# The scheduler's table of write tails, 300 cycles longer for VectorE and ScalarE, in a hybrid scan and MLP block

## The chip, the core and the metric

The kernel runs on one core of one Trainium2 chip. A core has five engines with queues of their own, each of which takes its instructions in the order of the program: PE (TensorE, matrix products, with its weight loads shown as PEld), DVE (VectorE), ACT (ScalarE), POOL (GpSimd) and SP (SyncE), which issues the transfers here. They wait for each other by semaphores. The metric is the time of one execution on the device in microseconds; lower is better.

## The reference

One layer of a generator's trunk works on 256 context tokens and 2048 latent tokens of width 1024. A modulated norm and one projection over all 2304 tokens give the columns of four mixers (mLSTM, RWKV-7, GLA, Gated DeltaNet; four heads each). Each mixer runs a forward and a backward scan over chunks of 64 tokens, 36 chunks in all, the context first. Their outputs go through one output projection, a gated residual, a second norm, an MLP with a squared ReLU and a last norm.

```python
mod_x = jax.nn.silu(c) @ ada_w[layer] + ada_b[layer]
...
hx = _rms(x, norm1_w[layer]) * (1 + scale1_x) + shift1_x
hc = _rms(ctx, norm1_w[layer]) * (1 + scale1_c) + shift1_c
z = (jnp.concatenate([hc, hx], axis=1) @ w_in[layer]).astype(jnp.float32)
z_ml, z_rw, z_gl, z_gd = _split(z, (ML_W, RW_W, GL_W, GD_W))
mixed = jnp.concatenate([
    _mlstm_mixer(z_ml, ...), _rwkv_mixer(z_rw, ...),
    _gla_mixer(z_gl, ...), _gdn_mixer(z_gd, ...)], axis=-1)
x = x + gate1_x * (mixed[:, n_ctx:] @ w_out[layer])
x = x + gate2_x * _mlp(_rms(x, norm2_w[layer]) * (1 + scale2_x) + shift2_x, ...)
...
return _rms(x, final_norm_w)
```

Two of the scans (RWKV-7 and Gated DeltaNet) solve a unit triangular system of 64 x 64 for each chunk, head and direction before their state can run:

```python
sol = lax.linalg.triangular_solve(-m_ab, rhs, left_side=True, lower=True, unit_diagonal=True)
...
def step(s, xs):
    w_c, u_c, a_c, k_c, v_c, ge = xs
    u_t = u_c + jnp.einsum('bhck,bhkv->bhcv', w_c, s)
```

## The kernel before

All dense products are made in three passes over split numbers (high by high, high by low, low by high), so a weight goes from its load `w_f` to `w_hi` on ACT and `w_lo` on POOL or DVE, and an activation to `hh` and `hl`.

**Stages.** Tokens are projected in five rounds (`round_`). A round begins with `make_h` (L533): for each of eight slices of 128 features, `xh` is loaded, multiplied by the norm's factor `rbr` on POOL, scaled on ACT, copied to `hh` on ACT, and `hl` is the rest on DVE; then PE makes the first product `ps_z`. After it come gates, the Gated DeltaNet's keys, the scalars, the RWKV columns (with `l2r` and `abrk` on POOL) and the columns of the other two. What the scans need goes to scratch in DRAM (`x_fm`, `x_tm`, `x_rows`, `x_gat`), from where a scan group (`group`) loads one chunk and one direction, runs its steps `ps_R`, `ps_U`, `ps_S`, `ps_att`, `ps_ym`, `ps_ylgr` and updates the state `St`. Four products for gates (`out_gates`), each with a `make_h` of its own, follow the rounds; a tail of output projection and MLP (`ps_o`, `ps_f`, `ps_a`) for four blocks of 512 tokens ends the program. 24 more groups stand in it.

**Solves.** `solve` serves four units (two chunks each). A `solve_prep` loads factors from `x_fm`, makes `ps_n` on PE and stores the system to `x_sN`. `find` loads it back (`s_s_b<-x_sN`) and inverts it in 31 steps of a product `s_t` and a subtraction into `s_s_x`, each on the result of the one before, on POOL (seven of the solves) or on DVE (solves of the last round, called `beside`). A `solve_post` makes two blocks of `ps_s` with ACT copies and stores the inverse to `x_t`, which the groups read. `s_s_b` and `s_s_x` are one buffer each, shared with the loads `adaw` of round 0's modulation and with `fill` (L349), which stores columns of ones into `x_tm`, four bytes at a time.

**What sets the order.** The program's text is interleaved by hand: a generator yields the pieces of a round, and `interleave` puts queued solves and groups between them.

```python
f = (i + 1 - lo * n) / ((hi - lo) * n)
want = min(len(steps), int(len(steps) * f)) if f > 0 else 0
...
r = _run(nc, [arrays], core_ids=[0])
```

On this the list scheduler of the tile framework works: it keeps a clock for each engine by tables of costs, and issues next what is ready first by these clocks. So the order on each engine, and nothing else of the program, depends on the tables. `transfers` (L1898) sets three entries of the tables for the time of scheduling and puts them back: the fixed cost of an SP transfer, its delay, and the bytes per ns of a DMA engine. The table the change adds to them gives, by kind of write of DVE and ACT, the cycles after an operation's end before the scheduler takes its result to be readable by another instruction.

Of the kernel before, what the change touches and what calls it, by code (L numbers as in the profile page):

```python
# [1897 lines left out]
@contextmanager  # L1898
def transfers():

    SP = mybir.EngineType.SP
    new = {"HWDGE_FIXED_OVERHEAD_NS": {**TRN2Spec.HWDGE_FIXED_OVERHEAD_NS, SP: 825},
           "DGE_DMA_DELAY": {**TRN2Spec.DGE_DMA_DELAY, SP: 1400},
           "DMA_BUS_BYTES_PER_NS_PER_ENGINE": 16.0}
    old = {k: getattr(TRN2Spec, k) for k in new}
    for k, v in new.items():
        setattr(TRN2Spec, k, v)
    try:
        yield
    finally:  # L1910
        for k, v in old.items():
            setattr(TRN2Spec, k, v)
# [15 lines left out]
```

## Time and profile before

| what | before |
|---|---|
| median of 3 runs | 4183.04 us (4180.95 to 4185.43) |
| the profiled execution | 4181.71 us |
| its span | 4179.9 us |
| mean granted clock of PE | 0.875 of full speed |
| busy: PE, DVE, ACT, POOL | 3462.1, 2490.3, 1403.3, 1464.4 us |
| moved by DMA | 592.66 MB, 142 GB/s on average |

By its landmarks in the trace the span falls into round 0 (to about 330 us), rounds 1 to 4 (to 1777), a stretch between two of the gates' dense pieces (to 1916 with its last hops), the rest of the gates (to 2280) and the tail. In the rows of the profile that follow, a timeline row gives the start and the duration in us, the engine, the line, the operation with what it writes and reads, and in brackets how long the engine had been idle and what released it. A window row gives, for each engine, the us in which it was busy and the number of instructions, then PE's granted clock, the busy share of the DMA engines and GB/s.

### The profile page before, as it was taken

The numbers are of one execution on the slowest core, as the hardware profiler recorded it, in microseconds if no ns is written. First come the engines' busy times: TensorE is split into PE (matmuls) and PEld (weight loads), VectorE is DVE, ScalarE is ACT, GpSimd is POOL, SyncE is SP. The second block draws the span as 40 slices with busy tenths as digits, with TensorE's granted clock in tenths as the row PEclk, the third lists the DMA queues.
The fourth block names the chain that finished last, engine by engine and source line by source line (L and its number), as shares of the span: only waits on it lengthen the run. The fifth ranks groups of instructions, "written<-read, shape, count | busy, mean of one in ns | idle before, by whom it ended". The sixth has DMA issues, their size and how long they took to land.

```text
span 4179.9 us, 75082 instructions
## 1 busy us (share of the span) xinstructions
PE 3462.1 (83%) x29082; PEld 2807.3 (67%) x29082; DVE 2490.3 (60%) x5259; ACT 1403.3 (34%) x2544; POOL 1464.4 (35%) x1682
## 2 busy tenths in 40 slices
PE   6465877867777876658896999999999999999998
PEld 5344666656556765547785777777778777877786
DVE  6673866764776585536865556567754464445444
ACT  3334334434433433323332323233322332233222
POOL 3221834552626253502242333334322232223222
PEclk9667978877887876768898999999999999999999
DMA  5568478657686864647777444454532333232322
GB/s 205 108 180 149 116 157 194 143 131 146 153 150 160 187 144 124 171 121 193 212 212 195 124 135 148 138 171 142 175 95 96 106 102 115 96 98 91 104 96 86
DMA packets 610372, 592.66 MB, mean 142 GB/s; under 512 B 286384, under 2 KB 487168, under 8 KB 610016
## 3 DMA queue, kind: packets, MB, share of 16 engines
q1 hardware_dynamic: 610016, 587.87, 53.9%
q8 instruction: 229, 3.75, 0.4%
q14 instruction: 127, 1.04, 0.1%
HBM read 463.78 MB, written 123.92 MB: 141 GB/s over the span
## 4 chain that ended last, share of the span: by engine, by line
PE 42%; DVE 4%; issue 1%; POOL 1%; ACT 1%; DMA 1%; SPq 0%; POOLq 0%; DVEq 0%; ACTq 0%
PE ps_a L240 17%; PE ps_f L240 15%; PE ps_o L240 4%; PE ps_ylgr L229 1%; PE ps_z L212 1%; PE ps_S L229 1%; PE ps_att L240 1%; DVE h2l L193 1%; DVE relu L185 1%; PE ps_R L229 1%; SPq L201 0%; PE ps_ym L229 0%; PE ps_yT L248 0%; PE ps_ml L240 0%; POOL yall L185 0%
## 5 line engine op out<-in xcount | busy, mean ns | idle before, releaser
L185 POOL TENSOR_TENSOR w_lo<-w_f,w_hi 128x1024 fp32r<-128x1024 f32 x213 | 513.9, 2413 | 1232.8 <-ACT w_hi L198 1144.1
L198 ACT ACTIVATE w_hi<-w_f 128x1024 fp32r<-128x1024 f32 (+1 forms) x427 | 448.5, 1051 | 878.1 <-PE ps_a L240 387.1
L240 PE MATMUL ps_a<-ah,w_hi 128*128 128x512 f32 x1024 | 408.0, 403 | 8.0 <-ACT ah L198 8.0
L240 PE MATMUL ps_f<-h2l,w_hi 128*128 128x512 f32 x1024 | 402.8, 394 | 8.7 <-DVE h2l L193 8.7
L185 DVE TENSOR_TENSOR w_lo<-w_f,w_hi 128x1024 fp32r<-128x1024 f32 (+1 forms) x214 | 275.0, 1285 | 222.4 <-ACT w_hi L198 218.2
L240 PE MATMUL ps_f<-h2h,w_hi 128*128 128x512 f32 x1024 | 404.4, 395 | 3.5 <-ACT w_hi L198 2.7
L240 PE MATMUL ps_a<-al,w_hi 128*128 128x512 f32 x1024 | 406.2, 397 | 1.0 <-DVE al L185 1.0
L240 PE MATMUL ps_f<-h2h,w_lo 128*128 128x512 f32 x1024 | 405.5, 396 | 1.1 <-DVE w_lo L185 1.1
L240 PE MATMUL ps_a<-ah,w_lo 128*128 128x512 f32 x1024 | 399.9, 398 | 0.0
L240 PE MATMUL ps_z<-hh,w_hi 128*128 128x512 f32 (+3 forms) x760 | 301.7, 403 | 73.7 <-ACT hh L198 34.2
L193 DVE SCALAR_TENSOR_TENSOR x1T<-ps_a,modv,x1T 128x512 f32<-128x512 f32 x256 | 188.0, 749 | 259.6 <-PE ps_a L240 258.9
L240 PE MATMUL ps_z<-hh,w_lo 128*128 128x512 f32 (+3 forms) x760 | 299.4, 395 | 21.2 <-DVE w_lo L185 11.0
L240 PE MATMUL ps_z<-hl,w_hi 128*128 128x512 f32 (+3 forms) x760 | 298.3, 393 | 2.1 <-DVE hl L185 1.9
L185 DVE TENSOR_TENSOR relu<-relu 128x512 f32<-128x512 f32 x128 | 188.4, 1473 | 113.0 <-ACT relu L198 112.9
L212 PE MATMUL ps_z<-w_hi,hh 128*128 128x256 f32 x672 | 210.3, 315 | 36.0 <-ACT hh L198 21.9
L240 PEld LDWEIGHTS ps_a<-ah,w_hi 128*128 128x128 f32 x1024 | 191.2, 189 | 64.7 <-ACT ah L198 16.5
L240 PEld LDWEIGHTS ps_z<-hh,w_hi 128*128 128x128 f32 (+1 forms) x760 | 155.2, 206 | 111.5 <-ACT hh L198 37.5
L240 PEld LDWEIGHTS ps_f<-h2l,w_hi 128*128 128x128 f32 x1024 | 193.9, 189 | 51.7 <-DVE h2l L193 10.7
L240 PEld LDWEIGHTS ps_f<-h2h,w_hi 128*128 128x128 f32 x1024 | 194.0, 190 | 46.0 <-ACT w_hi L198 4.4
L240 PEld LDWEIGHTS ps_a<-ah,w_lo 128*128 128x128 f32 x1024 | 193.4, 189 | 45.5 <-issue 0.3
L240 PEld LDWEIGHTS ps_a<-al,w_hi 128*128 128x128 f32 x1024 | 193.6, 189 | 44.8 <-DVE al L185 1.2
L240 PEld LDWEIGHTS ps_f<-h2h,w_lo 128*128 128x128 f32 x1024 | 193.9, 189 | 43.5 <-DVE w_lo L185 1.9
(430 smaller groups left out, 7976.9 us busy)
## 6 DMA issues: line engine op xcount, KB each, us to landing
w_f<-w SPq DMA_DIRECT2D x256, 512.0 KB
w_f<-wg SPq DMA_DIRECT2D x90, 512.0 KB
tm<-x_tm SPq DMA_DIRECT2D x144, 259.5 KB
kc<-x_fm SPq DMA_DIRECT2D x64, 448.0 KB
adaw<-ada SPq DMA_DIRECT2D x48, 512.0 KB
rw<-x_rows SPq DMA_DIRECT2D x144, 160.0 KB
w_f<-wp SPq DMA_DIRECT2D x44, 512.0 KB
w_f<-wout SPq DMA_DIRECT2D x32, 512.0 KB
```

The costliest lines, as they stand in the source:

```text
L185: return (e or self.V).tensor_tensor(out=o, in0=a, in1=b, op=op)
L193: return self.V.scalar_tensor_tensor(o, a, s, b, op0, op1)
L198: return self.S.activation(o, a, f, bias=bias, scale=scale)
L212: i = self.T.matmul(o, l, r, start=k == 0, stop=k == len(mms) - 1)
L229: i = self.T.matmul(t.t[rows, cols], l, r, start=not prev, stop=not any(left[q] for q in quarters), skip_group_check=True)
L240: return self.T.matmul(o, l, r, start=start, stop=stop)
```

## The change

A fourth table is set while the program is scheduled. Each of its eight entries, all of DVE or ACT, is raised by 300 cycles.

```diff
     new = {"HWDGE_FIXED_OVERHEAD_NS": {**TRN2Spec.HWDGE_FIXED_OVERHEAD_NS, SP: 825},
            "DGE_DMA_DELAY": {**TRN2Spec.DGE_DMA_DELAY, SP: 1400},
-           "DMA_BUS_BYTES_PER_NS_PER_ENGINE": 16.0}
+           "DMA_BUS_BYTES_PER_NS_PER_ENGINE": 16.0,
+
+           "TIMELINE_SIM_WRITE_TAIL_CYCLES": {k: v + 300 for k, v in TRN2Spec.TIMELINE_SIM_WRITE_TAIL_CYCLES.items()}}
     old = {k: getattr(TRN2Spec, k) for k in new}
     for k, v in new.items():
         setattr(TRN2Spec, k, v)
```

The instructions are the same in number and kind on every engine (PE 20456 matmuls in the order's count, DVE 5213, ACT 2546, POOL 1687, SP 2641); their order differs on all five. The mean place of an instruction moves by 85 on PE, 31 on DVE, 14 on ACT, 19 on POOL and 24 on SP. From about 3100 us of the trace of before on, the order is the same. Solves and scan groups stand earlier among the rounds, by 15 to 70 of PE's rows, and dense products later by 8 to 30, until the third of the gates' products, where both orders meet again.

**SP, end of round 0.** In the order of before, the four stores of ones by `fill` (`x_tm<-s_s_x 64x36x1`) stand behind the last load of `adaw` and the first weights `w_f` of the next product, and ahead of the loads of round 1's first solve (`s_s_b<-x_fm`) and of the next gate's weights:

```order
L201 DMA adaw<-ada 128x1024
L201 DMA x_tm<-tm 128x2x64
L201 DMA kc<-x_fm 128x128
L201 DMA ff<-x_fm 128x128
L201 DMA kc<-x_fm 128x256
L201 DMA kc<-x_fm 128x128
L201 DMA x_tm<-tm 128x2x128 x4
L201 DMA w_f<-wp 128x1024 x2
L201 DMA x_tm<-s_s_x 64x36x1 x4
L201 DMA s_s_b<-x_fm 128x2x128 x3
L201 DMA kc<-x_fm 128x256
L201 DMA s_s_x<-x_bg_90 64x2x256 x2
```

In the order of the change they stand among the stores of round 0's RWKV columns:

```order
L201 DMA adaw<-ada 128x1024
L201 DMA mf_bi<-x_msc_93 16x64
L201 DMA x_fm<-abrk 128x3x128
L201 DMA x_rows_89<-mf_re 4x4x64 x2
L201 DMA x_tm<-st 256x1x128
L201 DMA x_tm<-st 128x1x128
L201 DMA x_tm<-vt 256x1x64
L201 DMA x_tm<-vt 128x1x64
L201 DMA x_tm<-s_s_x 64x36x1
L201 DMA x_gat<-s_2243 256x1x128
L201 DMA x_gat<-s_2243 128x1x128
L201 DMA x_tm<-s_s_x 64x36x1 x3
```

The last `adaw` is SP's row 215 in the one and 184 in the other; the stores of ones moved from row 223 to rows 192 and 195.

**POOL, the last `find` on this engine.** In the order of before it begins when all `abrk` of round 4 and two updates of the state are behind it:

```order
L185 TENSOR_TENSOR abrk<-rmix,E 128x3x64
L1024 COPY reg<-E 128x3
L185 TENSOR_TENSOR w_lo<-w_f,w_hi 128x1024
L185 TENSOR_TENSOR s_17072<-vt,bon 128x4x64
L185 TENSOR_TENSOR s_17072<-s_17072,rgn 128x4x64
L185 TENSOR_TENSOR St<-St,rw 128x128
L185 TENSOR_TENSOR St<-St,reg 128x128
L185 TENSOR_TENSOR St<-St,rw 128x128
L185 TENSOR_TENSOR St<-St,reg 128x128
L1302 MEMSET s_s_x 128x1024
L1303 MEMSET s_s_x 128x32
L185 TENSOR_TENSOR s_t<-s_s_b,s_s_x 128x31
```

In the order of the change it begins behind the third-last and last `l2r`, with three `abrk` still to come:

```order
L1002 MEMSET E 128x3
L185 TENSOR_TENSOR abrk<-rmix,E 128x3x64
L1024 COPY reg<-E 128x3
L185 TENSOR_TENSOR l2r<-l2m,mhalf 128x6
L1302 MEMSET s_s_x 128x1024
L185 TENSOR_TENSOR St<-St,rw 128x128
L185 TENSOR_TENSOR St<-St,reg 128x128
L1303 MEMSET s_s_x 128x32
L185 TENSOR_TENSOR w_lo<-w_f,w_hi 128x1024
L185 TENSOR_TENSOR l2r<-l2m,mhalf 128x6
L185 TENSOR_TENSOR s_t<-s_s_b,s_s_x 128x31
L185 TENSOR_TENSOR s_s_x<-s_s_x,s_t 128x31
```

The `find` moved ahead of three `abrk`, of the bonus terms and of state updates; the eight `xh` of the first gates, which stand inside its last third before, stand behind it now. Elsewhere on POOL, `xh` rows come to stand inside other `find`s: of the rows of a `find`, 13 stand between the first and the last `xh` of round 3 and 7 between those of the gates before, and after 10 in round 1, 13 in round 2 and 18 in round 4. Up to the last `xh` of these three, 22, 13 and 49 rows of the `find` have gone by.

**PE, between the gates' second and third dense product.** In the order of before, the dense product `ps_z` ends and two blocks of `ps_s` of a `solve_post` follow, the first of four posts between here and the next `ps_z`, 132 rows on:

```order
L212 MATMUL ps_z<-w_lo,hh 128x256
L212 MATMUL ps_z<-w_hi,hl 128x256
L247 MATMUL ps_col<-pack,mf_m 64x32 x2
L247 MATMUL ps_col<-pack,mf_bi 64x16 x2
L240 MATMUL ps_s<-s_s_b 32x32 x16
L247 MATMUL ps_col<-pack,mf_ee 64x16 x2
L240 MATMUL ps_s<-s_s_x 32x32 x16
L229 MATMUL ps_ym<-St,Lq 64x65 x4
L229 MATMUL ps_ym<-tm,Lt 64x65 x4
```

In the order of the change the first `ps_n` of the next solve stands inside the dense product, and behind its end come steps of a group; until the next `ps_z`, 84 rows on, no `ps_s` stands:

```order
L229 MATMUL ps_R<-tm,Lt 64x64
L240 MATMUL ps_n<-s_s_b 64x64 x16
L240 MATMUL ps_ml<-kc 64x128 x2
L229 MATMUL ps_R<-tm,Lt 64x64 x3
L229 MATMUL ps_R<-St,ff 64x64 x4
L229 MATMUL ps_R<-St,kw 64x64 x4
L212 MATMUL ps_z<-w_hi,hh 128x256
L212 MATMUL ps_z<-w_lo,hh 128x256
L212 MATMUL ps_z<-w_hi,hl 128x256
L247 MATMUL ps_col<-pack,mf_ee 64x32 x2
L247 MATMUL ps_col<-pack,mf_m 64x32 x2
L240 MATMUL ps_ml<-kc 32x128 x2
```

All eight blocks of `ps_s` moved ahead of the second dense product's end.

## The prediction

> **What bounds the kernel now.** I read the busy times by stretch first, because a share over the whole span mixes stages with different limits.
>
> ```profile
> core 0: us, PE busy (x) PEld busy (x) DVE busy (x) ACT busy (x) POOL busy (x), PEclk, DMA share, GB/s
> 0.00:330.00 330.00, 186.04 (x931) 153.01 (x932) 224.21 (x622) 102.72 (x225) 96.16 (x168) 0.77 0.62 164
> 330.00:1777.00 1447.00, 1062.98 (x10517) 858.35 (x10515) 942.94 (x2165) 558.43 (x1127) 661.57 (x990) 0.78 0.69 152
> 1777.00:1916.00 139.00, 77.85 (x1367) 70.23 (x1368) 60.91 (x208) 30.31 (x86) 7.82 (x21) 0.66 0.54 133
> 1916.00:2280.00 364.00, 297.05 (x4888) 264.02 (x4886) 236.27 (x677) 129.06 (x268) 117.23 (x132) 0.89 0.74 203
> 2280.00:3100.00 820.00, 798.29 (x6927) 626.12 (x6928) 520.88 (x1054) 248.97 (x408) 296.35 (x237) 0.98 0.49 146
> 3100.00:4180.00 1080.00, 1039.90 (x4457) 835.54 (x4456) 505.12 (x535) 333.75 (x431) 285.29 (x137) 0.98 0.30 99
> ```
>
> From 2280 us on PE is busy for 798.29 of 820 and 1039.90 of 1080 us: no order of the other engines wins much there. Before that PE stands idle for 144 us in round 0 (330 - 186.04), 384 in rounds 1 to 4 (1447 - 1062.98), 61 in 139 between 1777 and 1916, and 67 in the rest of the gates. In 1777 to 1916 no engine is busy for more than 56% of the time (PE, 77.85 of 139): that stretch waits on chains. In the rounds nothing is full either, PE least idle with 73%. So an order can win up to some 650 us in principle, all before 2280; what it does win must come from named waits. Those of PE and POOL in the rounds (total us, times, longest):
>
> ```profile
> PE ps_ke L248 <- DVE ke L185: 63.7, 18, 8.5
> PE ps_z L240 <- ACT hh L198: 34.2, 8, 11.6
> PE ps_rb L248 <- ACT rb L198: 32.3, 14, 5.2
> PE ps_U L240 <- DVE gR L185: 14.5, 7, 4.7
> POOL xh L185 <- DMA xh<-xT: 57.4, 7, 24.7
> ```
>
> They are small and many; none is a fifth of the 384 us.
>
> **The change part by part.** No instruction comes or goes, so no duration is added or removed. The scheduler is told that a result of DVE or ACT is readable 300 cycles later, so it puts other work between such a result and its reader, on all five queues. In the tail from about 3100 us on nothing moves: 0. Three moves I can price.
>
> *A. The fill (SP).* Four stores of ones with four-byte elements stand in the order of before at the head of the round, ahead of that round's loads:
>
> ```profile
> 324.45 0.35 SPq L201 DMA_DIRECT2D adaw<-ada  x1
> 335.92 12.54 SPq L201 DMA_DIRECT2D x_tm<-s_s_x  x4
> 348.88 4.58 SPq L201 DMA_DIRECT2D s_s_b<-x_fm  x3
> ...
> 340.00:360.00 20.00, 3.51 (x15) 2.70 (x15) 3.50 (x5) 7.62 (x13) 2.35 (x1) 0.60 0.99 62
> ```
>
> Issuing them takes 12.54 us of SP, and in the 20 us after 340 the DMA engines are 0.99 busy at only 62 GB/s while PE works 3.51 us and the others at most 7.62. Everything waits for this. After the change the four stand 31 rows earlier on SP, among the last stores of round 0, ahead of several of them. There DVE has its longest share of any stretch (224.21 of 330), so part of the flood lies beside work and part delays round 0's own last stores. At most PE's idle time in that window goes (-16.5, 20 - 3.51), at least nothing (0). Nothing in the trace says how much of the flood the end of round 0 covers, so I take the middle, **-8**.
> The Trainium skill says under "DMA: Bandwidth & Descriptors", section "Rules for kernel authors", that a strided or non-contiguous last dimension is lowered to one descriptor per element. This trace agrees as far as it can, with a share of 0.99 at 62 GB/s, and by that rule the flood is as long wherever it is issued; if none of it were covered in its new place, the sum below would be 8 us higher.
>
> *B. Round heads (POOL).* Each round begins with eight `xh` on POOL, from which ACT makes `hh` and PE its first dense product. A `find` of the solves is 62 dependent POOL rows:
>
> ```profile
> L185 POOL TENSOR_TENSOR s_t<-s_s_b,s_s_x x217: 232/615/2572, 423.3 to 1768.8; 128x31 f32<-128x31 f32 x8, 128x87 f32<-128x87 f32 x8, 128x135 f32<-128x135 f32 x8, 128x175 f32<-128x175 f32 x8
> L185 POOL TENSOR_TENSOR s_s_x<-s_s_x,s_t x217: 247/647/3556, 423.9 to 1769.1; 128x31 f32<-128x31 f32 x8, 128x87 f32<-128x87 f32 x8, 128x135 f32<-128x135 f32 x8, 128x175 f32<-128x175 f32 x8
> ...
> 404.78 9.29 POOL L185 TENSOR_TENSOR xh<-xh,rbr 128x512 f32<-128x512 f32 x6 [3.20 <-DMA xh<-xT]
> ...
> 1748.45 1.26 POOL L185 TENSOR_TENSOR xh<-xh,rbr 128x512 f32<-128x512 f32 x1
> 1749.67 0.58 POOL L185 TENSOR_TENSOR s_s_x<-s_s_x,s_t 128x207 f32<-128x207 f32 x1
> 1750.22 1.27 POOL L185 TENSOR_TENSOR xh<-xh,rbr 128x512 f32<-128x512 f32 x1
> ```
>
> The median rows are 0.615 and 0.647 us, 0.631 on average. Before, two heads have find rows between their first and last `xh`: round 3 (13) and the gates (7, from 1748.45 on). After, three have them: round 1 (10), round 2 (13) and round 4 (18). That is 41 against 20, so 21 x 0.631 = **+13 us** if PE has nothing else at these heads. The 404.78 row shows six `xh` of round 1 in one go, without a find row between them. Bounds: 0, if the older products of the round before last until then, and all 41 rows, +26, if the two heads that get free of them win nothing. I take 13: the wait `ps_z <- hh` with 34.2 us in 8 says that PE does wait at heads.
>
> *C. The last POOL find.* It moves about 95 us ahead in POOL's queue:
>
> ```profile
> 1611.16 1.32 POOL L185 TENSOR_TENSOR l2r<-l2m,mhalf 128x6 f32<-128x6 f32 x1 [3.67 <-DVE mf_me L1134]
> ...
> 1650.50 0.55 POOL L185 TENSOR_TENSOR abrk<-rmix,E 128x192 f32<-128x192 f32 x1 [4.59 <-ACT E L198]
> ...
> 1700.66 0.40 POOL L185 TENSOR_TENSOR St<-St,rw 128x128 f32<-128x128 f32 x1 [23.07 <-PE ps_ylgr L229]
> ...
> 1707.95 0.24 POOL L185 TENSOR_TENSOR s_t<-s_s_b,s_s_x 128x31 f32<-128x31 f32 x1 [5.43 <-DMA s_s_b<-x_sN]
> ...
> 1769.11 0.25 POOL L185 TENSOR_TENSOR s_s_x<-s_s_x,s_t 128x31 f32<-128x31 f32 x1
> ```
>
> Before, it starts at 1707.95, after 23.07 us of POOL idling for a scan step and a wait for its input; after, it follows `l2r`, in the place that runs at 1611, and three `abrk` (0.55 us each) stand inside it. What is queued behind the find's first wait there is those `abrk`: they may come late by one landing, 5.43 us, but POOL has 23.07 us of idle time right behind them. So 0 for itself, at worst +5.4; its worth is in the next part.
>
> *D. The stretch behind it (PE).* The find's four results are turned into solutions by four `solve_post`, each two blocks of `ps_s`, a copy on ACT and a store, and the scan groups read those:
>
> ```profile
> 1774.99 0.28 PE L212 MATMUL ps_z<-w_hi,hl 128*128 128x256 f32 x1
> ...
> 1777.67 0.31 PE L240 MATMUL ps_s<-s_s_b 32*32 32x32 f32 x2 [0.15 <-ACT s_s_b L198]
> ...
> 1797.07 1.06 PE L240 MATMUL ps_s<-s_s_x 32*32 32x32 f32 x32
> ...
> 1819.79 0.31 PE L240 MATMUL ps_s<-s_s_b 32*32 32x32 f32 x2 [8.51 <-DMA s_s_b<-x_sN]
> ...
> 1832.80 1.92 PE L240 MATMUL ps_n<-s_s_b 64*64 64x64 f32 x32
> ...
> 1899.39 0.58 PE L212 MATMUL ps_z<-w_hi,hh 128*128 128x256 f32 x1
> ...
> 1824.50 0.45 SPq L201 DMA_DIRECT2D x_t<-s_s_b  x1
> 1800.00:1820.00 20.00, 5.18 (x102) 4.34 (x98) 3.40 (x11) 5.06 (x15) 1.21 (x4) 0.59 0.31 75
> ```
>
> Before, the dense work of one gate stops at 1774.99 and the next begins at 1899.39: 124 us, of which the posts take 1777.67 to 1824.50, **47 us**, at a quarter of PE (5.18 of 20 us). The next solve's first `ps_n` comes only behind them, at 1832.80. After the change the stretch between the same two dense pieces has 84 rows on PE instead of 132, none of them a `ps_s`, and its first `ps_n` stands inside the dense piece ahead. So 47 us of chain leave. The work itself goes elsewhere: eight blocks of about 1.06 us on PE, 8 us, of which the idle 27% of PE in the rounds should hide some; I charge 5, so **-42**. By rows it would be 124 x (1 - 84/132) = 45, the same size. Bounds: -55, if the 8 us from the last store (1824.50) to that `ps_n` (1832.80) go as well and the moved work is hidden, and -20, if the posts lengthen what they now stand in by half of their 47 us. What is late next is the solve computed on DVE behind those four preps, which ends this stretch either way; it is not shortened.
>
> *E. Hops of the scan and `ke`.* `ke` is read by PE with under 1 us of PE's other rows between in 8 places instead of 11, while of the steps of the scan 12 instead of 7 have next to nothing between. A wait for `ke` is 63.7 / 18 = 3.5 us and one for `rb`, the nearest kind to a scan step, 32.3 / 14 = 2.3: 3 x 3.5 won and 5 x 2.3 lost, **0**, and for both signs about these 11 us as bounds.
>
> **The sum.** -8 + 13 - 42 = -37. The profiled execution took 4181.71 us (its span 4179.9 and 1.8 around it), so 4144.7; the median of the runs is 1.3 higher, so **4146 us**. The bounds of the terms that matter, -16.5 + 0 - 55 and 0 + 26 - 20, give 4111 to 4189 for this case.
>
> **The rivals.**
> *Nothing comes of it.* The work in the rounds is only shuffled: what leaves the stretch lengthens the rounds by the same amount, because every piece there waits for a chain of loads. For it: DVE, PE and DMA are each busy for 65 to 73% of the rounds, and 0.69 of DMA with many small transfers is not idle. Against it: POOL's 23.07 us of waiting just where the find goes. Time: 4183, within 8 us of before.
> *Slower: the finds block POOL ahead of `xh`.* POOL takes its rows in order. After the change 22, 13 and 49 find rows stand ahead of the last `xh` of rounds 1, 2 and 4. If the find's input lands late (as the 5.43 us at 1707.95), all of `xh` waits: 84 x 0.631 + 3 x 5.43 = 69 us, less the 13 that the two heads of before lose now, +56; with -8 and half of the stretch (-21) that is +27, or 4210. It decides from the point where PE's older rows run out before POOL reaches the last `xh`. For it, find rows here run slower under load:
>
> ```profile
> 423.27 0.42 POOL L185 TENSOR_TENSOR s_t<-s_s_b,s_s_x 128x31 f32<-128x31 f32 x1
> 424.68 0.72 POOL L185 TENSOR_TENSOR s_t<-s_s_b,s_s_x 128x60 f32<-128x60 f32 x1
> ...
> 1708.62 0.28 POOL L185 TENSOR_TENSOR s_t<-s_s_b,s_s_x 128x60 f32<-128x60 f32 x1
> 420.00:440.00 20.00, 16.62 (x95) 11.78 (x93) 17.92 (x27) 7.19 (x11) 17.80 (x22) 0.99 0.45 119
> 1700.00:1720.00 20.00, 12.23 (x256) 11.08 (x253) 9.56 (x29) 7.66 (x18) 10.96 (x23) 0.93 0.81 196
> ```
>
> The same 128x60 row takes 0.72 us where DVE is busy for 17.92 of 20 us and 0.28 where it is for 9.56, and the first window is a round's head: that is why this rival gets a quarter and not a tenth. The Trainium skill, "SBUF — State Buffer", section "Who interferes with whom", says that DVE and GpSimd share one pair of ports under an exclusive lock, and the trace, with this ratio of 2.6, agrees.
> *A larger gain.* The change is aimed at exactly the waits for ACT and DVE that the rounds show: 63.7 + 34.2 + 32.3 + 14.5 = 145 us. If a third of them goes beside the sum, -48 more: 4098.
> *It doesn't do what it says.* Excluded: the orders differ on all five engines.
>
> **How the numbers follow.** Forecast 0.45, larger gain 0.20, nothing 0.12, slower by the finds 0.23. The predicted time is the forecast's, 4146. The range reaches from a little below the larger gain to the slower rival, 4085 to 4212, which leaves out some of both ends, about 0.16; the forecast's own range is 4111 to 4189. A measurement of this kernel can tell about 0.2%, 8 us. Of the forecast 0.05 lies within that, so faster is 0.40 + 0.20 = 0.60, within 0.2% is 0.05 + 0.12 = 0.17, and slower 0.23.
>
> **What would show it.** A: the four stores of ones come before 330 us and no window of 20 us after 330 has DMA at 0.99 with PE at a sixth. B: `xh` rows at three heads spread over more than 15 us, and the wait of `ps_z` for `hh` grows from 34.2. C and D: the last POOL find ends before 1700 on a clock set by the rounds, and the time between the two dense pieces falls from 124 to about 80 us with no `ps_s` in it. E: the sum of `ps_ke` and `ps_rb` in the rounds stays at 96 ± 11. The forecast is wrong if the rounds, from the fill to the first gate, last longer by more than 30 us, or if the stretch does not shorten.

## The result and the profile after

| | before | after |
|---|---|---|
| median of 5 runs | 4180.95 us (4168.29 to 4185.43) | 4199.39 us (4196.19 to 4204.97) |
| the profiled execution, its span | 4181.71, 4179.9 us | 4204.97, 4203.2 us |
| granted clock of PE | 0.875 | 0.869 |
| busy PE, DVE | 3462.1, 2490.3 us | 3486.6, 2467.2 us |

The ratio is 1.0054, with a 95% interval from 1.0039 to 1.0069: half a per cent slower, where 37 us less had been forecast.

Because only the order differs, both traces can be laid on each other at places where both orders have issued the same work. Some places differ by no more than a dozen instructions on all engines together; the trace of before passes them at 401, 1893, 2114, 2233 and 3054 us (the end of the last PE instruction ahead of the place). The next two fences are windows of before and of after, cut at these places; the columns are those of the windows in the prediction.

```profile
0.00:401.00 401.00, 221.68 (x1216) 183.45 (x1218) 245.73 (x668) 132.46 (x282) 100.60 (x172) 0.75 0.65 157
401.00:1893.00 1492.00, 1086.85 (x11396) 880.50 (x11394) 961.40 (x2259) 554.57 (x1145) 663.50 (x1003) 0.77 0.67 151
1893.00:2114.00 221.00, 191.16 (x3030) 173.36 (x3027) 157.66 (x451) 83.25 (x174) 54.69 (x64) 0.88 0.75 202
2114.00:2233.00 119.00, 102.16 (x1776) 90.92 (x1775) 83.53 (x239) 43.79 (x90) 56.59 (x59) 0.96 0.66 190
2233.00:3054.00 821.00, 774.36 (x6762) 607.28 (x6762) 512.61 (x1054) 244.24 (x405) 290.91 (x240) 0.96 0.52 153
3054.00:4180.00 1126.00, 1085.90 (x4919) 871.78 (x4917) 529.40 (x589) 344.95 (x449) 298.12 (x146) 0.98 0.30 99
```

```profile
0.00:400.00 400.00, 224.56 (x1218) 185.09 (x1218) 241.08 (x668) 128.29 (x275) 99.83 (x171) 0.76 0.67 157
400.00:1892.00 1492.00, 1096.30 (x11395) 887.69 (x11394) 954.22 (x2256) 560.14 (x1152) 658.55 (x1003) 0.77 0.67 152
1892.00:2130.00 238.00, 194.32 (x3013) 176.68 (x3013) 157.54 (x445) 82.47 (x174) 55.86 (x63) 0.85 0.67 185
2130.00:2270.00 140.00, 110.11 (x1792) 97.60 (x1788) 85.22 (x248) 43.70 (x90) 56.05 (x62) 0.86 0.58 166
2270.00:3093.00 823.00, 783.03 (x6760) 606.93 (x6759) 500.02 (x1054) 242.78 (x405) 284.50 (x238) 0.96 0.53 152
3093.00:4203.00 1110.00, 1078.24 (x4921) 871.03 (x4919) 529.11 (x589) 344.97 (x449) 301.42 (x146) 0.99 0.30 100
```

The counts of PE agree within 17 in every row, so each pair of rows is the same work. Every term to which the prediction gave a value other than 0 lies in the first two rows, and there the two orders come out even: 401 against 400 us and 1492 against 1492. The loss is in the next two, the gates: 221 to 238 and 119 to 140, 38 us. The tail from 3054 us on gives 16 back (1126 to 1110).

Inside the first two rows the moves can be seen, and each is paid back on the spot. This is SP's timeline after the change at the fill, with a window row behind it:

```profile
315.10 0.59 SPq L201 DMA_DIRECT2D x_tm<-s_s_x  x1
...
317.54 5.85 SPq L201 DMA_DIRECT2D x_tm<-s_s_x  x3
...
320.00:340.00 20.00, 5.63 (x20) 4.35 (x21) 4.06 (x13) 3.82 (x9) 0.19 (x1) 0.50 1.37 62
```

Three of the four stores start 18 us earlier than all four did before (317.54 against 335.92), and the window behind them is the same picture as before: 62 GB/s, PE busy for 5.63 of 20 us. (A share above 1, as the 1.37 here, means that the times of packets overlap; the share adds them up.) The next timelines after the change are PE's around the stretch between the gates' second and third product, and POOL's last find:

```profile
1829.83 0.28 PE L212 MATMUL ps_z<-w_hi,hl 128*128 128x256 f32 x1
1830.06 0.27 PE L240 MATMUL ps_n<-s_s_b 64*64 64x64 f32 x1
...
1832.43 0.28 PE L212 MATMUL ps_z<-w_hi,hl 128*128 128x256 f32 x1
...
1897.65 0.58 PE L212 MATMUL ps_z<-w_hi,hh 128*128 128x256 f32 x1
...
1698.75 0.24 POOL L185 TENSOR_TENSOR s_t<-s_s_b,s_s_x 128x31 f32<-128x31 f32 x1
...
1744.20 0.45 POOL L185 TENSOR_TENSOR s_s_x<-s_s_x,s_t 128x31 f32<-128x31 f32 x1
```

The stretch is 65 us long (1832.43 to 1897.65), where it was 124, with no `ps_s` in it. But it ends at the same time as before, 1897.65 against 1899.39: the dense product ahead of it has become late by what the stretch became shorter. Two windows of each kernel, split where the fifth round's `hh` comes, show where the time went:

```profile
405.00:1425.00 1020.00, 787.02 (x7522) 620.32 (x7522) 689.68 (x1537) 398.82 (x782) 492.09 (x735) 0.81 0.71 153
1425.00:1940.00 515.00, 334.84 (x4312) 292.95 (x4300) 299.51 (x802) 167.90 (x387) 178.75 (x277) 0.72 0.61 149
```

```profile
419.00:1511.00 1092.00, 837.18 (x8194) 664.14 (x8194) 722.70 (x1617) 406.62 (x806) 506.29 (x759) 0.79 0.68 151
1511.00:1945.00 434.00, 294.52 (x3604) 257.15 (x3604) 258.79 (x715) 160.96 (x362) 154.44 (x238) 0.71 0.63 153
```

708 PE instructions left the second window (4312 to 3604) and 81 us with them; 672 more stand in the first, and it takes 72 us more. Moved work costs 0.11 us an instruction in both places. (The windows end in the gates, at 1940 and 1945 us, so their sums are not those of the places.)

### The profile page after: what moved, and what is told of

The parts are those of the page before. It is cut to its first block, busy times and chain, and to the rows that moved or that the text cites. A ratio compares the mean times of both kernels' runs of the same rounds, so it can differ in the third digit from the quotient of the medians.

```text
span 4203.2 us, 75052 instructions
## 1 busy us (share of the span) xinstructions
PE 3486.6 (83%) x29082; PEld 2825.0 (67%) x29082; DVE 2467.2 (59%) x5259; ACT 1402.4 (33%) x2544; POOL 1456.2 (35%) x1682
## 4 chain that ended last, share of the span: by engine, by line
PE 44%; DVE 3%; DMA 2%; issue 2%; POOL 1%; SPq 1%; ACT 1%; POOLq 0%; DVEq 0%; ACTq 0%
PE ps_a L240 17%; PE ps_f L240 16%; PE ps_o L240 4%; PE ps_z L212 2%; PE ps_ylgr L229 1%; SPq L201 1%; PE ps_S L229 1%; PE ps_att L240 1%; DMA tm<-x_tm 1%; DMA rw<-x_rows 1%; PE ps_yT L248 0%; PE ps_R L229 0%; DVE w_lo L185 0%; PE ps_ym L229 0%; PE ps_U L240 0%
## 5 line engine op out<-in xcount | busy, mean ns | idle before, releaser
L185 DVE TENSOR_TENSOR w_lo<-w_f,w_hi 128x1024 fp32r<-128x1024 f32 (+1 forms) x214 | 266.4, 1245 | 219.2 <-ACT w_hi L198 215.9
L185 DVE TENSOR_TENSOR relu<-relu 128x512 f32<-128x512 f32 x128 | 190.8, 1492 | 125.2 <-ACT relu L198 125.2
```

What stands on the lines that cost most here:

```text
L185: return (e or self.V).tensor_tensor(out=o, in0=a, in1=b, op=op)
```

## The experiments

Two kinds of kernels ran. In the first, the order is given instead of found. Added edges make every engine issue all its instructions in a list; the lists are put together from the orders of before and of the change at the places above, so the instructions, their waits and what is computed stay the same. All `h_` kernels and x_hoist have this code and differ in QUEUES alone (it is shortened here):

```diff
+def pin(tc, nc):
+    ...
+    ins = {i.name: i for i in nc.cur_bb.bb.instructions}
+    for s in seqs:
+        s = [x for x in s if x in ins]
+        for a, b in zip(s, s[1:]):
+            tc.add_manual_dep(ins[b], a, ORDER, reason="order")
...
             body(ctx, tc, A, out)
+            pin(tc, nc)
```

In the second kind, the `t_` kernels, the table of write tails alone has other numbers. These kernels ran on two chips, h_end, h_tail, x_hoist and h_best on the one and the others on the other. On both before takes 4144 to 4148 us, where it took 4181 on the chip of the result; the ratios are to runs of before made with them. The table has the ratios with their intervals and the time between the places in the profiled execution of each (us; for the kernels with other tables, and for h_best up to 1893, a place is where the last PE instruction that lies ahead of it in before has ended). The first two rows are from the chip of the result, the first chip below; the change itself did not run on the two later chips. On these the order of before takes 392 us to the first place (h_gates, h_tail) and 1467 to 1480 us from there to the second (h_gates, h_tail, h_round0), and with these numbers the rows below compare.

| kernel | ratio | to 401 | to 1893 | to 2114 | to 2233 | to 3054 | to the end |
|---|---|---|---|---|---|---|---|
| before | 1 | 401 | 1492 | 221 | 119 | 821 | 1126 |
| the change | 1.0054 (1.0039 to 1.0069) | 400 | 1492 | 238 | 140 | 823 | 1110 |
| h_gates | 1.0092 (1.0073 to 1.0110) | 392 | 1467 | 234 | 139 | 812 | 1123 |
| h_rounds | 0.9960 (0.9945 to 0.9974) | 381 | 1462 | 220 | 120 | 821 | 1126 |
| h_round0 | 1.0010 (0.9998 to 1.0022) | 387 | 1480 | 220 | 120 | 815 | 1124 |
| h_notgates | 0.9937 (0.9923 to 0.9950) | 385 | 1459 | 221 | 118 | 820 | 1111 |
| t_act | 1.0045 (1.0029 to 1.0060) | 378 | 1481 | 246 | 110 | 822 | 1126 |
| t_dve | 0.9982 (0.9968 to 0.9995) | 398 | 1440 | 249 | 124 | 809 | 1123 |
| t_100 | 0.9935 (0.9912 to 0.9958) | 382 | 1443 | 232 | 125 | 811 | 1124 |
| t_600 | 1.0272 (1.0239 to 1.0305) | 417 | 1504 | 252 | 143 | 837 | 1110 |
| h_end | 0.9980 (0.9966 to 0.9994) | 384 | 1459 | 232 | 122 | 821 | 1110 |
| h_tail | 0.9959 (0.9943 to 0.9976) | 392 | 1472 | 219 | 122 | 819 | 1110 |
| x_hoist | 0.9959 (0.9943 to 0.9975) | 379 | 1474 | 220 | 122 | 825 | 1111 |
| h_best | 0.9870 (0.9849 to 0.9890) | 380 | 1446 | 223 | 120 | 821 | 1110 |

### Which stage loses

**h_gates**

> The order of before on all engines, except that between the places that the trace of before reaches at 1893 and 2233 us the order of the change stands. Theory G (the loss sits in the gates, where the change took 37.9 us longer between these two places): about 4181 + 38 = 4219, less what the tail gives back as it did in the change (from +37 to +23 at the end, 14), so 4205 to 4219. Rival R (the loss comes from the finds and heads of the rounds, and what differs later is only the chip's own spread): 4181, within 6.

Measured 4184.55 us against 4144.49, a ratio of 1.0092, 38 us more (30 to 46 by the interval). Theory G holds, at the upper end of its range; the tail gave nothing back, as it had the order of before.

**h_rounds**

> The order of the change up to the place at 1893 us of before, that of before from there on. G: the two traces stand at 1893 and 1892 us there, so 4180, within 6. R: 4199 or more, as the rounds bring all of the loss.

Measured 0.9960, 17 us faster. R falls. The order of the change up to 1893 us, even with that of before on the first chip, is a small gain here.

**h_round0**

> The order of the change only up to the place at 401 us of before (round 0 with the fill), that of before behind it. If the fill is moved but costs what it cost: the traces stand at 401 and 400 us, so 4180, within 6. If the earlier fill is a gain that the rest of round 0 only happened to lose (14 us at the last common place ahead of it), the time is below 4175.

Measured 1.0010, no change. Round 0 with the moved fill takes what it took. The fill alone was not moved in any run.

**h_notgates**

> The order of the change everywhere except between the places at 1893 and 2233 us of before, where that of before stands. G: 4199 - 38 = 4161 if the tail's gain of 14 belongs to the order, 4175 to 4181 if that gain belongs to the chip. R: 4199.

Measured 0.9937, 26 us faster than before. Only the gates stand between the change and a gain. In this the tail's gain belongs to the order, as one branch of G had it. The windows of the gates, first with the order of the change (h_gates), then with that of before (h_notgates), differ by 13 and 21 us, where the change and before differed by 17 and 21:

```profile
1859.00:2093.00 234.00, 192.43 (x3019) 175.40 (x3018) 156.23 (x445) 82.65 (x174) 56.51 (x63) 0.85 0.68 189
2093.00:2232.00 139.00, 109.92 (x1790) 97.38 (x1786) 85.37 (x248) 43.70 (x90) 55.92 (x62) 0.87 0.56 167
```

```profile
1844.00:2065.00 221.00, 190.00 (x3023) 172.66 (x3020) 161.59 (x453) 82.97 (x174) 55.32 (x64) 0.87 0.74 202
2065.00:2183.00 118.00, 101.69 (x1778) 90.43 (x1777) 82.29 (x239) 43.79 (x90) 55.85 (x59) 0.97 0.66 192
```

### Why the gates lose

PE's timeline at the end of the gates, in before: the last dense product and what `ps_yT` (an output of the groups) follows it.

```profile
2212.03 0.28 PE L212 MATMUL ps_z<-w_hi,hl 128*128 128x256 f32 x1
...
2220.82 0.55 PE L248 MATMUL ps_yT<-pack,yall 128*128 128x128 f32 x3 [1.34 <-POOL yall L185]
...
2232.82 0.55 PE L248 MATMUL ps_yT<-pack,yall 128*128 128x128 f32 x3 [2.02 <-POOL yall L185]
```

And after the change:

```profile
2229.37 0.28 PE L212 MATMUL ps_z<-w_hi,hl 128*128 128x256 f32 x1
...
2244.10 1.42 PE L248 MATMUL ps_yT<-pack,yall 128*128 128x128 f32 x4 [4.04 <-POOL yall L185]
...
2256.91 1.42 PE L248 MATMUL ps_yT<-pack,yall 128*128 128x128 f32 x4 [2.97 <-POOL yall L185]
...
2269.32 1.42 PE L248 MATMUL ps_yT<-pack,yall 128*128 128x128 f32 x4 [6.02 <-POOL yall L185]
```

From 2114 to the last dense product both need 98 us (2130 to 2229 after). Then the chain of the groups goes on alone, with `yall` made on DVE and POOL between the PE pieces, at 12 to 13 us a step. Before, two of these outputs are left up to the place, after three, and the first comes 14.7 us after the dense product instead of 8.8. In the order, 38 blocks of the groups' `ps_ylgr` stand ahead of the last dense product before and 36 after. I read this so: the scheduler, which takes each result of DVE and ACT as later, put the dense rows into the gaps of the chain sooner, and ran out of them one output sooner. The same at the end of the third product, on PE after the change:

```profile
1934.29 0.28 PE L212 MATMUL ps_z<-w_hi,hl 128*128 128x256 f32 x1
...
1940.45 0.31 PE L240 MATMUL ps_s<-s_s_b 32*32 32x32 f32 x2 [4.83 <-ACT s_s_b L198]
...
1945.29 0.58 PE L212 MATMUL ps_z<-w_hi,hh 128*128 128x256 f32 x1 [1.00 <-ACT hh L198]
```

Here two blocks of `ps_s` stand behind the product's last row; before, the same blocks stood inside it (`ps_s` at 1927.62, `ps_z` to 1934.3). Up to this place, 1944 us here and 1935 in before, 10 of the 17 us are lost; where the other 7 go isn't traced.

Four other tables test this reading (LAG) against a mere lottery (L), in which the count of outputs says nothing.

```diff
-"TIMELINE_SIM_WRITE_TAIL_CYCLES": {k: v + 300 for k, v in ...}
+"TIMELINE_SIM_WRITE_TAIL_CYCLES": {k: v + 300 * (k[2] == mybir.EngineType.Activation) for k, v in ...}
```

**t_act** (above), **t_dve** (the same with DVE), **t_100** and **t_600** (100 and 600 cycles for all)

> 300 cycles for the four entries of ACT alone. On PE, 38 outputs of scan groups (ps_ylgr) stand ahead of the last dense product of the gates, as in the order of before (36 in the order of the change). Theory LAG (the gates lose because the dense products end before the groups, and what is left of the groups runs with nothing beside it): the part from 2114 to 2233 us of before takes about 120 us as before; the whole is 5 to 25 us faster than before on the same chip, as the rounds and the tail of the change were. Rival L (any other table gives another shuffle, and how many outputs are left says nothing): no relation, the part may take 140.

> 300 cycles for the four entries of DVE alone. 37 outputs stand ahead of the last dense product. LAG: the part from 2114 to 2233 us takes 125 to 135; the whole within 12 us of before. L: no relation.

> 100 cycles for all eight entries. 37 outputs stand ahead of the last dense product. LAG: the part takes 125 to 135; the whole within 12 us of before. L: no relation.

> 600 cycles for all eight entries. 36 outputs stand ahead of the last dense product and three blocks of ps_yT instead of four (before five). LAG: the part takes 140 or more; the whole 15 to 40 us slower than before. L: no relation.

The part from 2114 to 2233 us followed the outputs ahead: 110 us for t_act (38), 124 and 125 for t_dve and t_100 (37), 143 for t_600 (36), beside 119 (38) and 140 (36) of before and of the change. But with another table a part doesn't hold the same work: t_act has 1557 PE instructions in it and t_dve 1654, where before has 1776. The time from the last dense product of the gates to the first `ps_o` of the tail doesn't hang on these places, and it goes the same way: 50 us in before and 54 in t_act (38), 58 in t_100 and 67 in t_dve (37), 72 in the change and 77 in t_600 (36). For the whole time LAG missed three times: t_act was to be faster and is 0.45% slower, t_100 gained 0.65% where 12 us were allowed, and t_600 lost 109 us where 15 to 40 were expected. Most of this comes from other parts. t_act loses 25 us between 1893 and 2114, where the count at the end of the gates says nothing; t_100 gains in the rounds; t_600 loses in every part up to 3054. So LAG tells the part, not the kernel, and for the whole there is much of L: 100 cycles for all are a gain, 300 and 600 a loss.

**h_end** puts the order of before into that part alone.

> The order of the change everywhere except in the last part of the gates (2114 to 2233 us of before), where that of before stands: 38 outputs of groups ahead of the last dense product instead of 36. LAG: the part takes 119 instead of 139, and the whole 0.48% less than the change (1.0054), so a ratio of 1.001 to the time of before. Rival L: the part's time hangs on what comes before it, and the ratio stays at 1.005.

Measured 0.9980 (the part took 122 us). Beside 1.0054 that is 0.74%, more than the 0.48% expected, but the two ratios are from different chips; the part itself is 17 us shorter than the 139 of h_gates. So the order inside the part decides its time. Whether it is the count of outputs or something else in this order, h_end alone doesn't tell. The second of these windows, which are cut at whole microseconds, shows PE's granted clock with it, 0.91 where h_gates has 0.87:

```profile
1842.00:2074.00 232.00, 193.27 (x3015) 176.41 (x3013) 157.34 (x445) 82.45 (x174) 56.61 (x63) 0.85 0.68 189
2074.00:2197.00 123.00, 107.31 (x1791) 94.92 (x1787) 84.92 (x248) 43.78 (x90) 57.84 (x62) 0.91 0.67 191
```

### The tail and the heads

**h_tail** has the order of the change from 3054 us on and is that of before up to there.

> The order of before up to the place at 3054 us, that of the change from there on, where only a few rows of each weight block stand some places later. Theory T (the tail's order is worth something: PE meets no wait for ah any more, 8.0 us in the trace of before, 0.0 in that of the change): 10 to 14 us faster than before, a ratio of 0.997. Rival: the chip's own spread, a ratio of 1.000.

Measured 0.9959, 17 us faster (10 to 24 by the interval); the part itself takes 1110 us, 13 less than in h_gates: T holds. In the costliest groups of the profile, PE's product with `ah` (busy, mean ns, idle ahead of it and its releaser) reads in before and in h_tail:

```profile
L240 PE MATMUL ps_a<-ah,w_hi 128*128 128x512 f32 x1024 | 408.0, 403 | 8.0 <-ACT ah L198 8.0
```

```profile
L240 PE MATMUL ps_a<-ah,w_hi 128*128 128x512 f32 x1024 | 399.5, 401 | 2.6 <-ACT ah L198 2.6
```

In most weight blocks one to three of these rows stand some places later, so that PE meets `ah` when it is there or nearly so. All kernels with the order of the change in the tail need 1110 or 1111 us for it, all with that of before 1123 to 1126. The wait accounts for 5 of these 13 us. PE's busy time in the part is 6 us less (1083.81 in h_gates, 1078.14 in h_tail); the last 2 us aren't traced.

**x_hoist** is h_notgates with the find rows on POOL taken out from between the `xh` of rounds 1, 2 and 4. For round 4, told in words:

```diff
 POOL, round 4, the order
-xh, 11 rows of a find, xh, 2 rows, xh x2, 1 row, xh, 1 row, xh, 1 row, xh, 2 rows, xh
+xh x8, 18 rows of a find
```

> The order of h_notgates, and on POOL the rows of a find that stand between the first and the last xh of rounds 1, 2 and 4 (41 rows, 26 us) moved behind the last xh. Step B of the prediction: 13 to 26 us faster than h_notgates (0.9937), a ratio of 0.988 to 0.9906. Rival: the heads are covered by older products on PE, the ratio stays at 0.9937.

Measured 0.9959, against 0.9937 for h_notgates: nothing of the 13 to 26 us. (The intervals overlap, 0.9943 to 0.9975 and 0.9923 to 0.9950, and the chips differ, so a loss isn't shown either.) Round 4's `xh` now run within 11 us of each other (1466.9 to 1477.5, before that move 1464.2 to 1481.7), but the wait at the heads only changed its name: PE's wait of `ps_z` for `hh` falls from 18.1 to 10.8 us, and the one for `w_lo` grows by 20. PE's waits from the first head to the end of the stretch, in h_notgates and in x_hoist:

```profile
PE ps_z L240 <- POOL w_lo L185: 13.2, 7, 3.2
```

```profile
PE ps_z L240 <- POOL w_lo L185: 33.2, 8, 10.3
```

The rows of the find that gave way to `xh` now stand ahead of the weights' low parts. At round 4 POOL begins a `w_lo` at 1498.01 us, behind the find's second-last row at 1497.81, and PE stands for 10.3 us until it is done; the longest waits for `w_lo` at the heads of rounds 1 and 2 are 8.3 and 6.6 us. An order with the find behind these `w_lo` too was not run.

### A version that beats both

**h_best** takes the order of t_100 for the rounds, that of before for the gates and the first part of the tail, and that of the change for the rest.

> The order of t_100 up to the place at 1893 us of before, that of before up to 3054, that of the change behind it. If the parts add: t_100 stood at 1826 there where before stood at 1859 on this chip, the gates of before save 17 against t_100, the tail of the change 10 to 14: about 4148 - 33 - 12 = 4103 or a ratio of 0.989. If the parts hang on each other: above 0.993.

Measured 4095.02 us against 4148.04, a ratio of 0.9870: the parts add, to 53 us less.

## Why the prediction was wrong

The sum failed in two steps. The first is the one that turned the sign: it put the gates behind their third product at nothing (E), and they lost 38 us. The second is the charge of 5 us for the work that left the stretch (D), which came to 72.

**What bounds the kernel** was read rightly: all differences but the tail's lie in chains ahead of 2280 us.

**A, the fill (-8).** Measured about 0: up to 401 us the traces stand at 401 and 400, and h_round0 at 1.0010. The failed step is the choice of the middle between 0 and 16.5 us. The flood stops all engines at its new place as at the old one, so the end of round 0 covers none of it that can be measured. The Trainium skill has the rule, under "DMA: Bandwidth & Descriptors", section "Rules for kernel authors", that such a last dimension becomes one descriptor per element. The trace agrees with it: between 330 and 365 us of before 9869 packets are smaller than 512 bytes, and the four stores hold 9216 elements.

**B, the heads (+13).** The rows moved as described, and x_hoist, which took them away from between the `xh`, was no faster. The failed step is "if PE has nothing else at these heads": PE waits there for `w_lo` from the same POOL queue as well, and this wait takes over. That the sum of waits on `hh` would grow from 34.2 us was wrong too; in the rounds after the change the row is

```profile
PE ps_z L240 <- ACT hh L198: 14.3, 10, 5.1
```

**C, the find** moved ahead of the last `abrk` without harm, but it starts only 9 us earlier on the clock (1698.75 against 1707.95) and not 95, since what it stands behind has become later.

**D, the stretch (-42).** The shortening came, by 59 us and not 47. The failed term is the charge of 5 us for the work that left it: 672 PE instructions more in the first four rounds took 72 us there. On the later chip it is much the same, 1008 us from round 1's first `hh` to round 4's in h_gates and 1065 in h_rounds. I had counted the eight blocks of `ps_s` alone and hidden part of them in PE's idle 27%. But far more moved (a block of `ps_s` is 32 instructions, the eight 256), and most of it was not hidden. That the idle time belongs to chains which more work doesn't fill is my reading; no run tests it alone. B and D together came to 0 on the first chip and, by h_rounds and h_round0 (0.9960 against 1.0010), to a gain of about 21 us on the later chip, where 29 were forecast. Why the rounds gain on one chip and not on the other is open.

**E, the hops (0 ± 11).** This is the term that turned the sign. It priced a bare hop by PE's mean wait in the rounds. Even there it missed: the waits for `ke` and `rb` came to 77.5 us (44.0 and 33.5), not 96 ± 11. What the longer table costs is another thing: dense rows are spent earlier in the gaps of the chain, and what remains of the chain when they are spent runs uncovered. I had taken the two orders as meeting at the gates' third product and looked no further. They meet there as sets of instructions, but their interleaving goes on to differ, and h_gates shows 38 us for just that.

**The tail (0).** The account ahead of the prediction says that the order is the same from about 3100 us on. It is not: the engines hold the same work there at each step, with a few rows of each block exchanged. h_tail measures 17 us won by these, 13 of them inside the part.

**The rivals.** The slower one named the right sign and nearly the size (4210) for a wrong reason: the heads. The bound that I named for being wrong, rounds longer by more than 30 us, was met (419 to 1799 instead of 405 to 1751 between the heads, 34 us), although the shorter stretch made it good. The rival that nothing comes of it had the reason that holds for the first two rows on the first chip, that what leaves the stretch lengthens the rounds by the same amount; its time of 4183 was missed for the gates. The larger gain, that PE's waits for DVE and ACT fall, came in the rounds for `ke` (63.7 to 44.0 us) and `hh` (34.2 to 14.3) and didn't shorten them.

On the later chips the pieces of the change are -0.4% (rounds with round 0), +0.92% (gates) and -0.41% (tail), together +0.1%, if they add. On the first chip the whole is +0.54%, and its rounds gave nothing. This part of the difference isn't settled.

## What to carry to other kernels

Where a scheduler's table changes, compare the two orders stage by stage to the end, not to the first place where they hold the same work: the interleaving behind it may differ and cost more than all that moved ahead of it. At the end of each stretch of dense work, count what is left of the chains that it covered; each step left there is paid in full. Work that is moved out of an uncovered stretch can cost as much where it lands, unless the trace shows idle time there which it can really fill. And an order found by a table can be taken apart and put together again by stage.

## What was not expected of the hardware

The uncovered chain costs twice. In the last part of the gates PE does nearly the same matmuls (1776 and 1792 records) in 102.16 us at a granted clock of 0.96 (before) and in 110.11 us at 0.86 (after); in h_gates and h_notgates it is 109.92 at 0.87 against 101.69 at 0.97. So of the 21 us lost there 8 are slower matmuls and 13 more idle time. The change's trace shows when the clock falls, in windows around its first two waits ahead of `ps_yT`, of 4.04 and 2.97 us:

```profile
2233.00:2242.00 9.00, 6.10 (x196) 5.28 (x194) 5.11 (x24) 3.03 (x9) 3.17 (x2) 1.00 0.91 265
2242.20:2248.80 6.60, 4.18 (x57) 3.52 (x59) 2.37 (x8) 0.95 (x3) 3.08 (x6) 0.50 0.31 93
2249.00:2255.60 6.60, 3.91 (x113) 3.17 (x108) 4.85 (x20) 1.35 (x4) 1.65 (x1) 1.00 0.02 4
2255.80:2262.40 6.60, 4.63 (x60) 3.75 (x60) 1.58 (x5) 0.60 (x1) 2.72 (x5) 0.50 0.29 89
```

It is halved within each wait (the `ps_yT` behind them begin at 2244.10 and 2256.91) and stays so over the work that follows. The Trainium skill, "TensorE: Matmul & The Clock Gate", section "Part 1: The HAM clock gate", says that the clock falls to half after an idle window of some 3.4 us. The trace agrees in the fall to half; but the second wait, 2.97 us, is shorter than that, and the clock fell in it all the same.

The other surprise is the spread that the order alone makes: the same instructions took from 4095 us (h_best) to 4257 us (t_600), 4%, on two chips on which before takes 4148 us.
